# A hybrid decoder layer in fp32: the value half of the up weights is loaded into the other ring of weight buffers

## The chip, the core and the metric

The kernel runs on one core of one Trainium2 chip. The metric is device time in microseconds (us) of one execution; lower is better. All times below come from the timed runs or from one profiled execution. In the rows PE is TensorE, PEld its weight loads, DVE is VectorE, ACT is ScalarE, POOL is GpSimd, and SP is SyncE, which issues all DMAs here.

## What is computed

One decoder layer on 1024 tokens of width 1024: three token mixers (forgetting attention, a short gated convolution, a gated delta rule), merged into the residual, then a channel mixer, then a gated embedding per layer. The change touches the channel mixer alone:

```python
u = causal_dwconv(rmsnorm(x, g_ffn) @ w_up, ffn_conv_w)   # width 3, D_FF = 2816
u_gate, u_val = jnp.split(u, 2, axis=-1)
x = x + (jax.nn.silu(u_gate) * u_val) @ w_down
```

## The kernel before, in words

Activations lie transposed, 128 channels by 1024 tokens to a tile. Products run in two parts: each fp32 operand is split into a high part (a copy on ScalarE, L129) and a low part (a subtraction, L130, mostly on VectorE), and each product is three matmuls: high by high, high by low, low by high. A weight tile so split stands in the ring "wo" (5 buffers).

The up projection works through 22 pairs f of one gate tile and one value tile of 128 output channels each. The weights of a tile are 128 x 1024 fp32, 512 KB. Pairs 0 and 1 use the plain product (`plain`). Pairs 2 to 21 use a product by seven (`seven`, Strassen-Winograd's): the gate tile holds the blocks a11 and a12, the value tile a21 and a22, and `stationary` forms four sums of them,

- s1 = a21 + a22 on GpSimd, s2 = s1 - a11 on VectorE, s3 = a11 - a21 on GpSimd, s4 = a12 - s2 on VectorE (all L199),

in a ring "ws" of 3 buffers of 512 columns. Seven weights go to TensorE: a11 (product 1), a12 (2), s4 (3), a22 (4), s2 (6), s3 (7), s1 (5). A block of the loop takes seven products of 12 matmuls: in program order product 1 of the new pair, 3 of the old pair, 2 new, 4 old, then 6, 7, 5 new. So a22 and s4 of a pair are used a block later than its other weights. Results are evacuated on ScalarE (L213, L217, L227, L230) and VectorE (L220, L223, L231). When a pair is complete, `gated` runs the convolution's taps (L1092 on ScalarE, L1094 on VectorE), the sigmoid (L1125), the gate's product (GpSimd, L1126) and the value's (VectorE, L1128), and stores the activation tile to DRAM (L1133). Pairs 2 and 3 stay in SBUF.

Two rings of weight buffers of 128 x 1024 fp32 matter here:

- "wq", 3 buffers, filled by `wpair` (L192): in the up projection gate and value tile of each pair in turn, so a tile takes the buffer of the third tile before it. After the up projection `wpair` reads activations back (`fetch`).
- "wr", 2 buffers, filled by `wraw` (L136): the weights of all other products, the embedding's (wple) before the up projection and the down projection's (wdn) after it. In the up projection nothing uses it.

A buffer can be filled again when the last reader of its tile is done. For the value tile that is the split of a22; for the gate tile it is s4, which reads a12.

The order of instructions on each engine's queue isn't written by hand: a planner lays it out when the kernel is built, from modelled times of all instructions, in program order where two are ready. Each engine, SyncE's DMA queue too, then runs its own queue in that order and waits where an operand or a buffer isn't ready.

Of the kernel before, what the change touches and what calls it, by code (L numbers as in the profile page):

```python
# [17 lines left out]
NF = 22  # L18
# [30 lines left out]
def hybrid_block(ctx: ExitStack, tc: tile.TileContext, I, out, dbg=None):  # L49
    nc = tc.nc  # L50
    dbg = dbg or {}
    V, S, G, Q = nc.vector, nc.scalar, nc.gpsimd, nc.sync
    uid = [0]

    def nm(s):
        uid[0] += 1
        return f"{s}_{uid[0]}"
# [8 lines left out]
    @contextmanager  # L66
    def phase(name, psum=None, **roles):

        with ExitStack() as es:
            def pool(n, **k):  # L70
                return es.enter_context(tc.tile_pool(name=n, bufs=1, reuse_waits="tile", **k))
            sb = pool(name)
            ps = pool(name + "p", space=bass.MemoryType.PSUM) if psum else None
            old = dict(homes)
            homes.update({r: (sb, n) for r, n in roles.items()})
            homes.update({r: (ps, n) for r, n in (psum or {}).items()})
            scopes.append(sb)
            yield
            scopes.pop()
            homes.clear()  # L80
            homes.update(old)

    def pt(tag, bufs, w=512, dt=F32):
        pool, n = homes.setdefault(tag, (scopes[-1], bufs))
        return pool.tile([P, w], dt, tag=tag, name=nm(tag), bufs=n)
# [33 lines left out]
    def col(i):  # L119
        return cols[:, i : i + 1]  # L120
# [7 lines left out]
    def split(h, l, x, eng=None):  # L128
        S.activation(h, x, AF.Copy)  # L129
        (eng or V).tensor_tensor(out=l, in0=x, in1=h.bitcast(F32), op=ALU.subtract)  # L130
# [3 lines left out]
    def wraw(src, n=1024):  # L134
        wr = wp.tile([P, 1024], F32, tag="wr", name=nm("wr"), bufs=WR)
        Q.dma_start(wr[:, :n], src)  # L136
        return wr

    def wsplit(x, eng):

        m = x.shape[-1]
        w = wp.tile([P, 1024], F32R, tag="wo", name=nm("wo"), bufs=WO)
        h, l = w[:, 0:m], w[:, 512 : 512 + m]
        split(h, l, x, eng)
        return h, l

    def wload(src, n=1024, eng=None):
        wr = wraw(src, n)
        return [wsplit(wr[:, c : min(c + 512, n)], eng or weng[0]) for c in range(0, n, 512)]
# [26 lines left out]
    def operand(x, new):  # L176

        o = new()
        split(o[:, 0:512], o[:, 512:1024], x)
        return o  # L180

    def moving_sums(b1, b2, new, eng):

        x11, x12, x21, x22 = b1[:, NB[0]], b1[:, NB[1]], b2[:, NB[0]], b2[:, NB[1]]
        t3, t2, t4 = (pt("u", 4) for _ in range(3))
        for e, o, x, y in zip(eng, (t3, x12, t2, t4), (x22, x12, x22, x21), (x12, x11, x12, t2)):
            (G if e == "g" else V).tensor_tensor(out=o, in0=x, in1=y, op=ALU.subtract)
        return {6: operand(t2, new), 5: operand(x12, new), 7: operand(t3, new), 4: operand(t4, new)}

    def wpair(src, n=1024):  # L190
        w = pt("wq", 3, 1024)
        return w, Q.dma_start(w[:, :n], src).ins  # L192

    def stationary(a, b, m):

        a11, a12, a21, a22 = a[:, 0:m], a[:, m : 2 * m], b[:, 0:m], b[:, m : 2 * m]
        s1, s2, s3, s4 = (pt("ws", 3)[:, 0:m] for _ in range(4))
        for e, o, x, y, op in zip(SUMS, (s1, s2, s3, s4), (a21, s1, a11, a12), (a22, a11, a21, s2), (ALU.add,) + (ALU.subtract,) * 3):
            (G if e == "g" else V).tensor_tensor(out=o, in0=x, in1=y, op=op)  # L199
        return {k: lambda x=x, e=e: wsplit(x, G if e == "g" else V)  # L200
                for k, x, e in zip((1, 4, 2, 6, 3, 7, 5), (a11, a22, a12, s2, s4, s3, s1), SUBS)}
# [32 lines left out]
    def plain(ws, xs, outs):  # L234

        ps = [mmb() for _ in range(4)]
        for k in range(8):
            kt, half = k // 2, k % 2
            for m in range(2):
                wh, wl = ws[2 * m + half]  # L240
                sl = slice(kt * P, kt * P + P)
                for nb in range(2):
                    x = xs[half, nb][kt]
                    h, l, o = x[:, 0:512], x[:, 512:1024], ps[2 * m + nb]
                    mm(o, wh[:, sl], h, k == 0, False)
                    mm(o, wh[:, sl], l, False, False)
                    mm(o, wl[:, sl], h, False, k == 7)
        for o, p in zip(outs, ps):
            S.activation(o, p, AF.Copy)
# [698 lines left out]
    def xgt():  # L948
        return xp.tile([P, T], F32R, tag="xg", name=nm("xg"))

    def big(dt=F32):
        return pt("a", 16, T, dt)

    with phase("la", psum=dict(mm=6, sm=2), a=16, wq=3):
        with phase("me", tmp=9, sg=4, yr=4):
# [50 lines left out]
            for b in range(3):  # L1006
# [5 lines left out]
                for d2 in range(4):  # L1012
# [8 lines left out]
                    w = wload(I["wbr"][4 * b + d2])  # L1021
# [67 lines left out]
        with phase("up"):  # L1089
            def taps(cv, c0):  # L1090
                o = pt("o", 3, T)
                S.activation(o, cv[:, 0:T], AF.Copy, scale=col(c0))  # L1092
                for i in (1, 2):
                    V.scalar_tensor_tensor(out=o, in0=cv[:, i : i + T], scalar=col(c0 + i), in1=o,  # L1094
                                           op0=ALU.mult, op1=ALU.add)
                return o

            stored = []

            def padded():  # L1100
                cs = pt("cg", 2, T + 4), pt("cw", 2, T + 4)
                for c in cs:
                    G.memset(c[:, 0:2], 0.0)
                return cs

            def spans(*cs):
                return [c[:, 2 + 512 * nb : 514 + 512 * nb] for c in cs for nb in range(2)]

            acts, ahead = {}, {}

            def fetch(f):
                acts[f], ins = wpair(adr[f])
                return ins

            def gated(f, cg, cv):
                if f == NF - 1:
                    with tc.issue_after(stored[-1]):
                        for g in GROUPS[1][:3]:
                            fetch(g)
                        for dt in range(8):  # L1120
                            ahead[dt] = big()
                            Q.dma_start(ahead[dt], x2dr[dt])
                o = taps(cg, C_FF + 3 * f)
                sg = cg[:, 2 : T + 2]
                S.activation(sg, o, AF.Sigmoid)  # L1125
                G.tensor_tensor(out=sg, in0=o, in1=sg, op=ALU.mult)  # L1126
                o = taps(cv, C_FF + 3 * (NF + f))
                V.tensor_tensor(out=o, in0=o, in1=sg, op=ALU.mult)  # L1128
                if f in KEPT:
                    acts[f] = xgt(), xgt()  # L1130
                    split(*acts[f], o)
                else:
                    stored.append(Q.dma_start(adr[f], o).ins)  # L1133

            def up(f):
                w = stationary(wpair(I["wup"][f])[0], wpair(I["wup"][NF + f])[0], 512)
                cg, cv = padded()
                return w, spans(cg, cv), lambda: gated(f, cg, cv)

            halves = {(h, nb): [] for h in range(2) for nb in range(2)}  # L1140
            for k in range(4):
                for h in range(2):
                    x = x2s[k + 4 * h]
                    V.scalar_tensor_tensor(out=x, in0=x, scalar=col(C_G2 + k + 4 * h), in1=rs2, op0=ALU.mult, op1=ALU.mult)
                    for nb in range(2):
                        halves[h, nb].append(operand(x[:, NB[nb]], xgt))
            xs = {1: halves[0, 0], 2: halves[1, 0], 3: halves[1, 1], 4: [], 5: [], 6: [], 7: []}
            for f in range(PLAIN):
                cg, cv = padded()
                if f:  # L1150
                    wa, wb = wpair(I["wup"][f])[0], wpair(I["wup"][NF + f])[0]
                    first = [wsplit(x, V) for x in (wa[:, 0:512], wa[:, 512:1024], wb[:, 0:512], wb[:, 512:1024])]
                plain(first, halves, spans(cg, cv))
                gated(f, cg, cv)
                for k in (2 * f, 2 * f + 1):
                    for i, t in moving_sums(x2s[k], x2s[k + 4], lambda: big(F32R), "vvvv").items():
                        xs[i].append(t)
            seven([lambda f=f: up(f) for f in range(PLAIN, NF)], xs)

        with phase("do", tmp=8, sg=4):  # L1160
# [11 lines left out]
            for g in GROUPS:  # L1172
                for f in g:
                    act(f)
                n = len(g)
                for d2 in range(4):
                    w = wload(I["wdn"][:, c0 : c0 + 256 * n], 256 * n)
# [101 lines left out]
```

## Time and profile before

| | us |
|---|---|
| median of 3 runs | 1984.83 (1982.81 to 1985.93) |
| profiled execution | 1983.83 |
| its span, first to last instruction | 1981.7 |
| TensorE busy in it | 1938.0 |
| VectorE busy in it | 1337.2 |

The span lies inside the profiled execution's time. The seven-product loop stands from about 1251 to 1652 us. The granted clock of TensorE is 0.997 of full speed over the span.

### The profile page before, as it was taken

To read this page: it belongs to the slowest core of one execution; us is meant where nothing else is said; L and a number is where in the kernel's file an instruction comes from. 1 tells how busy PE (TensorE), PEld (TensorE's weight loads), DVE (VectorE), ACT (ScalarE), POOL (GpSimd) and SP (SyncE) were. 2 spreads that over 40 slices of the span, in tenths; PEclk is the share of its full clock that TensorE was granted. 3 is DMA by queue.
4 is the path that set the end of the run, shared out by engine and by line. 5 is a ranking of instruction groups with operands and counts; after the bars stand their busy time and mean duration, and the time that the engine had idled before them with its cause. 6 is when DMAs were issued, how large, how long until landed. Compare 5 with 4: busy or idle time off the path is not lost. (4 is left out here: it accounts for less than half of the span.)

```text
span 1981.7 us, 25403 instructions
## 1 busy us (share of the span) xinstructions
PE 1938.0 (98%) x9281; PEld 1608.2 (81%) x9281; DVE 1337.2 (67%) x2161; ACT 907.7 (46%) x1651; POOL 526.8 (27%) x431
## 2 busy tenths in 40 slices
PE   8999999999999999999999999999999999999998
PEld 6888888888888888888788787777777778888887
DVE  6878788878487123348757439888788888444564
ACT  6576777677422233333424336444444444111351
POOL 1445334434322222100044011334343430000200
PEclk9999999999999999999999999999999999999999
DMA  4221112221432144357853432121212127322132
GB/s 178 70 90 67 59 59 71 68 74 65 151 111 91 62 136 138 98 209 252 300 182 128 181 109 94 58 70 64 96 64 97 64 75 274 105 88 86 43 117 85
DMA packets 102636, 219.40 MB, mean 111 GB/s; under 512 B 9360, under 2 KB 40432, under 8 KB 102512
## 3 DMA queue, kind: packets, MB, share of 16 engines
q1 hardware_dynamic: 102512, 217.79, 32.4%
q8 instruction: 73, 1.20, 0.3%
q14 instruction: 51, 0.42, 0.1%
HBM read 158.98 MB, written 58.77 MB: 110 GB/s over the span
## 5 line engine op out<-in xcount | busy, mean ns | idle before, releaser
L126 PE MATMUL mm<-xg,wo 128*128 128x512 f32 x6128 | 1486.3, 393 | 18.4 <-DVE wo L130 12.3
L126 PEld LDWEIGHTS mm<-xg,wo 128*128 128x128 f32 x6128 | 1140.8, 188 | 262.1 <-DVE wo L130 19.5
L126 PE MATMUL mm<-a,wo 128*128 128x512 f32 x1216 | 303.6, 389 | 1.4 <-DVE sg L1029 1.4
L126 PEld LDWEIGHTS mm<-a,wo 128*128 128x128 f32 x1216 | 228.4, 188 | 49.7 <-DVE sg L1029 1.8
L129 ACT ACTIVATE wo<-wr 128x512 fp32r<-128x512 f32 x232 | 144.6, 626 | 267.3 <-PE mm L126 257.7
L130 POOL TENSOR_TENSOR wo<-wr,wo 128x512 fp32r<-128x512 f32 x108 | 149.8, 1390 | 312.8 <-ACT wo L129 301.8
L1181 DVE TENSOR_TENSOR a<-mm,a 128x512 f32<-128x512 f32 x96 | 65.2, 687 | 91.6 <-PE mm L126 91.4
L130 DVE TENSOR_TENSOR wo<-wr,wo 128x512 fp32r<-128x512 f32 x124 | 89.4, 723 | 28.0 <-ACT wo L129 27.4
L280 POOL TENSOR_TENSOR tmp<-tmp,tmp 128x512 f32<-128x512 f32 x21 | 28.1, 1339 | 293.4 <-ACT tmp L278 281.8
L1030 POOL TENSOR_TENSOR a<-a,sg 128x512 f32<-128x512 f32 x28 | 42.4, 1520 | 191.9 <-DVE sg L1029 191.9
L130 DVE TENSOR_TENSOR wo<-wq,wo 128x512 fp32r<-128x512 f32 x68 | 79.2, 1166 | 3.2 <-ACT wo L129 3.2
L1094 DVE SCALAR_TENSOR_TENSOR o<-cw,cols,o 128x1024 f32<-128x1024 f32 x44 | 77.8, 1768 | 0.0
L491 DVE SCALAR_TENSOR_TENSOR o<-cv,cols,o 128x512 f32<-128x512 f32 x72 | 69.9, 970 | 10.1 <-ACT o L489 9.1
L503 ACT ACTIVATE o<-mm 128x512 f32<-128x512 f32 x60 | 35.7, 595 | 89.4 <-PE mm L126 53.3
L129 ACT ACTIVATE wo<-ws 128x512 fp32r<-128x512 f32 x80 | 50.2, 631 | 56.8 <-PE mm L126 56.7
L600 ACT ACTIVATE pp<-pp,small 128x512 f32<-128x512 f32 (+2 forms) x96 | 58.4, 610 | 28.0 <-DVE small L594 27.6
L1126 POOL TENSOR_TENSOR cg<-o,cg 128x1024 f32<-128x1024 f32 x22 | 55.6, 2525 | 39.4 <-ACT cg L1125 39.4
L199 POOL TENSOR_TENSOR ws<-wq 128x512 f32<-128x512 f32 x20 | 29.9, 1494 | 122.6 <-DMA wq<-wup 121.4
L1092 ACT ACTIVATE o<-cw,cols 128x1024 f32<-128x1024 f32 x22 | 25.4, 1156 | 74.8 <-DVE cw L223 74.8
L130 DVE TENSOR_TENSOR pl<-pq,ph 128x512 fp32r<-128x512 f32 (+1 forms) x80 | 49.9, 628 | 13.9 <-ACT ph L129 13.5
L199 POOL TENSOR_TENSOR ws<-wq,wq 128x512 f32<-128x512 f32 x20 | 43.7, 2186 | 56.3 <-DVE wo L130 52.3
L199 DVE TENSOR_TENSOR ws<-ws,wq 128x512 f32<-128x512 f32 x20 | 14.9, 745 | 64.3 <-POOL ws L199 64.3
(291 smaller groups left out, 2453.4 us busy)
## 6 DMA issues: line engine op xcount, KB each, us to landing
wr<-win SPq DMA_DIRECT2D x64, 512.0 KB, 3.6
wq<-wup SPq DMA_DIRECT2D x44, 512.0 KB, 3.5
r<-o SPq DMA_DIRECT2D x64, 256.0 KB, 2.6
ad<-o SPq DMA_DIRECT2D x20, 512.0 KB, 3.9
wq<-ad SPq DMA_DIRECT2D x20, 512.0 KB, 4.4
wr<-wdn SPq DMA_DIRECT2D x20, 512.0 KB, 3.7
yr<-r SPq DMA_DIRECT2D x16, 512.0 KB, 5.1
sg<-r SPq DMA_DIRECT2D x32, 256.0 KB, 3.4
```

The costliest lines, as they stand in the source:

```text
L126: pe[0] = nc.tensor.matmul(o, lhsT=l, rhs=r, start=start, stop=stop, skip_group_check=more)
L129: S.activation(h, x, AF.Copy)
L130: (eng or V).tensor_tensor(out=l, in0=x, in1=h.bitcast(F32), op=ALU.subtract)
L199: (G if e == "g" else V).tensor_tensor(out=o, in0=x, in1=y, op=op)
L280: eng[nb].tensor_tensor(out=acc[nb], in0=acc[nb], in1=sq, op=ALU.add)
L491: V.scalar_tensor_tensor(out=o, in0=cv[:, i : i + 512], scalar=col(c0 + i), in1=o, op0=ALU.mult, op1=ALU.add)
L503: S.activation(o, ps, AF.Copy)
L600: S.activation(t[:, :w], t[:, :w], AF.Exp, bias=mn[:, k - 1 : k], scale=-1.0, accum_out=sm[:, i : i + 1])
L1030: (V if b == 2 and dt > 5 else G).tensor_tensor(out=m, in0=m, in1=t, op=ALU.add)
L1094: V.scalar_tensor_tensor(out=o, in0=cv[:, i : i + T], scalar=col(c0 + i), in1=o, op0=ALU.mult, op1=ALU.add)
L1126: G.tensor_tensor(out=sg, in0=o, in1=sg, op=ALU.mult)
L1181: V.tensor_tensor(out=x2[dt][:, NB[nb]], in0=ps, in1=x2[dt][:, NB[nb]], op=ALU.add)
```

## The change

The value tile of each pair from 2 to 21 is loaded by `wraw` into the ring "wr" instead of by `wpair` into the ring "wq"; the gate tile stays in "wq". Pairs 0 and 1 are loaded as before. `wpair` loses a parameter that no caller used. No buffer is added to either ring, and the sums, splits and products are the same.

```diff
-    def wpair(src, n=1024):
+    def wpair(src):
         w = pt("wq", 3, 1024)
-        return w, Q.dma_start(w[:, :n], src).ins
+        return w, Q.dma_start(w, src).ins
@@
             def up(f):
-                w = stationary(wpair(I["wup"][f])[0], wpair(I["wup"][NF + f])[0], 512)
+                w = stationary(wpair(I["wup"][f])[0], wraw(I["wup"][NF + f]), 512)
                 cg, cv = padded()
                 return w, spans(cg, cv), lambda: gated(f, cg, cv)
```

## Rows read from the trace of the kernel before

**Rows 1.** Page, busy time by engine: us, share of the span, instructions.

```profile
PE 1938.0 (98%) x9281; PEld 1608.2 (81%) x9281; DVE 1337.2 (67%) x2161; ACT 907.7 (46%) x1651; POOL 526.8 (27%) x431
```

**Rows 2.** Windows: stretch, length, busy us (instructions), granted clock, DMA share, GB/s.

```profile
1251.60:1273.33 21.73, 18.49 (x74) 14.49 (x72) 15.77 (x15) 7.34 (x13) 9.01 (x7) 0.92 0.18 66
1273.33:1292.37 19.04, 19.04 (x86) 15.77 (x84) 16.80 (x17) 10.13 (x15) 7.13 (x7) 1.00 0.20 60
...
1312.42:1631.26 318.84, 309.54 (x1345) 251.01 (x1344) 258.01 (x256) 146.85 (x224) 123.44 (x97) 1.00 0.22 78
```

**Rows 3.** Timeline of PE, one block: start, length, form, [idle before <-releaser].

```profile
1411.70 8.32 PE L126 MATMUL mm<-a,wo 128*128 128x512 f32 x36
...
1425.30 0.61 PE L126 MATMUL mm<-xg,wo 128*128 128x512 f32 x2
...
1426.42 5.28 PE L126 MATMUL mm<-xg,wo 128*128 128x512 f32 x22 [0.51 <-DVE wo L130]
```

**Rows 4.** Timeline of the same block: DVE, POOL and SP's queue.

```profile
1411.79 0.69 DVE L199 TENSOR_TENSOR ws<-wq,ws 128x512 f32<-128x512 f32 x1
...
1412.55 15.98 SPq L192 DMA_DIRECT2D wq<-wup  x2
...
1416.12 1.28 POOL L199 TENSOR_TENSOR ws<-wq 128x512 f32<-128x512 f32 x1 [4.91 <-DMA wq<-wup]
1417.44 0.69 DVE L199 TENSOR_TENSOR ws<-ws,wq 128x512 f32<-128x512 f32 x1 [3.70 <-POOL ws L199]
...
1423.89 2.48 DVE L130 TENSOR_TENSOR wo<-wq,wo 128x512 fp32r<-128x512 f32 x1
...
1427.49 0.68 DVE L130 TENSOR_TENSOR wo<-wq,wo 128x512 fp32r<-128x512 f32 x1
...
1429.33 0.33 SPq L1133 DMA_DIRECT2D ad<-o  x1
...
1431.65 0.69 DVE L199 TENSOR_TENSOR ws<-wq,ws 128x512 f32<-128x512 f32 x1
```

**Rows 5.** Waits, 1240 to 1680 us: waiter <- releaser: us, times, longest.

```profile
PE mm L126 <- DVE wo L130: 12.3, 17, 3.0
```

**Rows 6.** Groups by form, 1312 to 1632 us: busy us, mean ns | idle before.

```profile
L130 DVE TENSOR_TENSOR wo<-wq,wo 128x512 fp32r<-128x512 f32 x48 | 61.7, 1285 | 0.0
L1094 DVE SCALAR_TENSOR_TENSOR o<-cw,cols,o 128x1024 f32<-128x1024 f32 x32 | 57.5, 1798 | 0.0
L1126 POOL TENSOR_TENSOR cg<-o,cg 128x1024 f32<-128x1024 f32 x16 | 41.9, 2616 | 5.2 <-ACT cg L1125 5.2
L1094 DVE SCALAR_TENSOR_TENSOR o<-cg,cols,o 128x1024 f32<-128x1024 f32 x32 | 40.9, 1279 | 0.0
L130 DVE TENSOR_TENSOR wo<-ws,wo 128x512 fp32r<-128x512 f32 x48 | 40.7, 848 | 0.0
...
L199 POOL TENSOR_TENSOR ws<-wq,wq 128x512 f32<-128x512 f32 x16 | 36.4, 2276 | 51.2 <-DVE wo L130 51.2
...
L130 POOL TENSOR_TENSOR wo<-ws,wo 128x512 fp32r<-128x512 f32 x17 | 22.6, 1331 | 7.6 <-ACT wo L129 7.6
...
L199 POOL TENSOR_TENSOR ws<-wq 128x512 f32<-128x512 f32 x16 | 20.6, 1288 | 78.9 <-DMA wq<-wup 78.9
```

**Rows 7.** The up loads of line 192, 1312 to 1632 us: issue to landing.

```profile
DMA to landing us min/median/max: 3.3/3.6/4.1
```

**Rows 8.** Timeline at the start of the loop.

```profile
1233.29 1.76 DVE L199 TENSOR_TENSOR ws<-ws,wq 128x512 f32<-128x512 f32 x1 [1.18 <-POOL ws L199]
...
1263.38 3.68 PE L126 MATMUL mm<-xg,wo 128*128 128x512 f32 x8 [3.01 <-DVE wo L130]
```

**Rows 9.** Timeline around the end of the loop.

```profile
1176.84 0.33 SPq L136 DMA_DIRECT2D wr<-wdn  x1
...
1636.79 0.69 DVE L130 TENSOR_TENSOR wo<-wq,wo 128x512 fp32r<-128x512 f32 x1
...
1649.85 2.88 PE L126 MATMUL mm<-a,wo 128*128 128x512 f32 x12
```

## Prediction

> **What bounds the kernel now.** I read the busy table first: TensorE is busy 98% of the span [rows 1], so the whole kernel has 44 us of TensorE idleness to give back, and only what lies in the stage that the diff touches counts. Next I cut that stage, the seven-product loop of the up projection, into stretches [rows 2]. A product is 12 matmuls; five of them, without a hole, fill the 13.60 us from 1411.70 to 1425.30 [rows 3], so one product is 2.72 us and one block of seven is 19.04 us. The stretch of one block from 1273.33 lasts exactly that: a block without loss. The 16 blocks from 1312.42 to 1631.26 last 318.84 us, 19.93 each, so each loses 0.89 us, 14.2 us in all.
>
> Where a block loses it stands in the timeline of TensorE [rows 3]: two matmuls at 1425.30, which end their turn at 1425.75, then a hole of 0.7 us until VectorE has made the low half of a weight (1426.42, released by DVE wo L130). The list of waits names the same releaser, 17 times [rows 5]. So I asked why VectorE is late, and read its own timeline with those of GpSimd and SyncE [rows 4]. Call the block whose sums are made there f. VectorE makes s4 of block f-1 at 1411.79; this is the last read of the gate tile of f-1, and only now (1412.55) SyncE can issue the value load of f into its buffer. GpSimd stands idle 4.91 us for that load, makes s1 at 1416.12, and VectorE, which runs its queue in order, stands idle 3.70 us at s2 (1417.44) with three taps, an evacuation and two weight splits queued behind it, the last of them the one that TensorE needs. That split is the one at 1423.89.
>
> This is a loop: s4 on VectorE, load, s1 on GpSimd, s2 on VectorE, all other work of VectorE, the next s4. Its length is VectorE's work plus the idle time: 258.01 us over 16 blocks [rows 2] is 16.13 of work, and 19.93 less that leaves 3.8, which is the idle time at s2. TensorE needs 19.04 and gets 19.93: VectorE's loop, not TensorE, sets the pace.
>
> **The change part by part.** *Value loads in the other ring.* Removed: the value half's place in the three-buffer ring wq. Added: a place in the two-buffer ring wr. No instruction is added, none grows; the 44 up loads stay 512 KB each on SyncE's queue. What moves is the event that frees the buffer. Today the value tile of f+1 takes the buffer of the gate tile of f, freed by s4 of f (1431.65 to 1432.34). Changed, it takes the value buffer of f-1, last read by the split of its second half on VectorE, at 1427.49 [rows 4], which ends at 1428.17. That is 4.2 us earlier. A load of this stage lands in 3.3 to 4.1 us [rows 7], so it is there by 1432.3. The sum s1 of f+1 also needs a buffer of the three-deep ring ws, freed by the same s4, at 1432.34. The load is thus hidden behind a wait that exists anyway, and what is late next is s4 itself.
>
> From there GpSimd needs 1.29 us [rows 6], so s1 ends at about 1433.7. VectorE meanwhile has two pieces of about 0.6 us after s4 (an evacuation, a split of the next gate tile) and is free at about 1433.6. Its idle time falls from 3.8 us to some 0.2; its loop would be 16.13 + 0.2 = 16.3 us, under TensorE's 19.04, and the 0.89 us vanishes. With VectorE ahead by up to 3.6 us, the hole of 0.7 us at 1425.75 closes with 2.9 us to spare.
>
> What can eat that margin, bounded by rows: s1 no longer runs while VectorE is idle. At best it costs nothing; at worst VectorE is held for the whole 1.29 us and s1 itself grows to the 2.28 us of the equal sum s3 that runs beside VectorE [rows 6], 1.0 more. The loop is then 16.13 + 1.29 + 0.2 + 1.0 = 18.6, still under 19.04. I take 14.2 us of gain, and 0 for the worst, since no end crosses 19.04 by itself. If besides the planner puts the value load behind the activation store (issued at 1429.33 [rows 4], 1.1 us after the buffer is free, landing by about 1433.4), 0.9 us more would give 19.5, and only 0.43 of the 0.89 us would be won: a gain of 6.9. This is the low end.
>
> *Gate loads.* With the ring wq to themselves the gate tiles run three blocks deep: the load of f+2 is free to go at s4 of f-1, a whole block before use. Cost nothing, covered by some 19 us of lead. The two loads in a block simply swap places on SyncE's queue: the slot just ahead of the store is today a gate load's, and it still lands within 4.1 us [rows 7], so the store that follows it does not hold it up much.
>
> *Start of the loop.* From 1251.60 to 1273.33, six products (16.32 us) take 21.73: 5.4 us lost, 3.01 of them in one hole [rows 2, 8]. Here VectorE is full with the two plain blocks' taps and moving sums and waits for GpSimd's first sum only 1.18 us [rows 8], so an early value load can give at least 0, at most 5.4; nearest is the 1.18, and I take 1.2. The block between 1292.37 and 1312.42, the ends of its neighbours, lasts 20.05, 1.0 over [rows 2]; it waits in the same loop, I take 1.0 (0 to 1.0).
>
> *End of the loop and the down projection.* Today two down-projection weights sit in wr some 460 us ahead of use, the later one issued at 1176.84 [rows 9]. In the changed kernel the value tiles hold wr until the end, so the second of these loads waits for the split of the last value tile, today at 1636.79 [rows 9]. Issued at 1637.5 it lands by 1641.6, is split 1.3 us later, and its matmuls come after those at 1649.85: nothing lost. If the planner leaves that split until TensorE needs it, at 1649.85, the weight is ready at 1649.85 + 3.6 + 1.3 = 1654.8, and TensorE, done at 1652.57, waits 2.2 us. I take 0; bounds 0 and 2.2, no gain.
>
> **Sum.** 14.2 + 1.0 + 1.2 = 16.4 us. The profiled execution took 1983.83 us (span 1981.7, 2.1 around it): 1967.4. The median of the runs is 1.0 above it, so 1968.4.
>
> **The rivals.** *Part of it comes back* (chance 0.13): the load queued behind the store, or a planner's order in which VectorE still waits a microsecond or two. The time by the low end above: 14.2 shrinks to 6.9, the start gives 0, the end costs 0 to 2.2: 1984.8 - 6.9 + 2.2 = 1980 down to 1974. For it: the order is made by a planner from modelled times that I do not see. Against: the slot in which the load would stand is used today without delay.
>
> *Nothing changes* (0.09): the planner, knowing the load early, puts s1 or s2 elsewhere and VectorE waits as long for something else, for instance s3, for which GpSimd already idles 51.2 us over 16 blocks, 3.2 each, behind VectorE [rows 6]. VectorE's loop stays near 19.9 and the time near 1984.8. Against: no other row makes VectorE wait in a steady block; it idles once.
>
> *Slower, by VectorE and GpSimd holding each other up* (0.07). VectorE's work of 16.13 us already holds some of this: splits from wq average 1285 ns where an undisturbed one is 0.68, taps of cw 1798 where those of cg take 1279, splits from ws 848 [rows 6]. Over a block that is 3 x 0.60 + 2 x 0.52 + 3 x 0.17 = 3.35 us, beside 6.22 us of GpSimd (2.28 + 2.62 + 1.33): about half. Undisturbed, VectorE would need 12.8. With s1 all four GpSimd pieces, 7.5 us, would lie beside VectorE. Were it held for all of them, the loop would be 20.3, 0.37 over today, 16 times: +5.9, so 1990.7. It decides from the point where VectorE is held for more than 19.93 - 12.8 = 7.1 of those 7.5 us. Against: half, not all, is what the rows show.
> The Trainium skill's "SBUF — State Buffer" (section "SBUF: two separate sides") says that these two engines share one pair of ports under an exclusive lock, and that the one that comes second blocks for the whole instruction. By that rule alone this rival would be the forecast; the half that the trace shows goes against reading it so strictly.
>
> **How the numbers follow.** Forecast 0.71, 1964 to 1974: its best end takes all of the start, 14.2 + 1.0 + 5.4 = 20.6 off 1984.8, so 1964.2. The range reaches down to 1963 and up over the partial case to 1979; outside stay the unchanged and the slower case and a little below, under 2 in 10. A measurement of this kernel can tell about 0.2%, 4 us, from no change. Faster by more: 0.71 and 0.13, 0.84; same 0.09; slower 0.07.
>
> **What the changed profile would show.** Right: the idle time of GpSimd before ws<-wr L199 released by a load gone, or released by VectorE; VectorE's idle time before s2 under 1 us; blocks of 19.04 in TensorE's timeline and no hole after two matmuls; value loads issued right behind the split of the second half. Wrong: blocks still near 19.9 with VectorE busy for more than 18 us of each (held by GpSimd), or idle elsewhere (a new wait), or a hole of several us at the first down-projection weights. The whole fails if the hole after two matmuls stays though VectorE no longer waits at s2.

## The result and the profile after

| | before | after |
|---|---|---|
| median, us | 1982.81 (run beside it) | 1967.19 |
| ratio after to before, 95% interval | | 0.9913 (0.9900 to 0.9927) |
| profiled execution, us | 1983.83 | 1967.07 |
| its span, us | 1981.7 | 1965.1 |

The medians differ by 15.6 us, which is 0.79%; the ratio, with its interval, says 0.87%. Four of the five runs of the changed kernel lie between 1966.51 and 1967.22; a fifth, of 3942.92, is left out of the ratio. The spans differ by 16.6 us. The page's busy table after:

```profile
PE 1930.3 (98%) x9281; PEld 1605.9 (82%) x9281; DVE 1331.0 (68%) x2161; ACT 910.8 (46%) x1651; POOL 531.9 (27%) x431
```

Windows of the stretches that answer to those of before [rows 2]: start to the first three products of the second pair, the block that lost 1.0, and the 16 steady blocks (stretch, length, busy of PE, PEld, DVE, ACT, POOL with instructions, granted clock, DMA share, GB/s).

```profile
1250.68:1270.41 19.73, 17.27 (x74) 13.28 (x72) 15.33 (x15) 6.23 (x11) 6.89 (x6) 1.00 0.15 54
1289.45:1308.49 19.04, 19.04 (x86) 15.77 (x84) 16.04 (x17) 10.12 (x15) 7.79 (x6) 1.00 0.14 51
1308.49:1613.13 304.64, 304.64 (x1346) 252.25 (x1344) 254.63 (x258) 150.10 (x224) 120.21 (x97) 1.00 0.23 79
```

The 16 steady blocks last 304.64 us, 19.04 each, and TensorE is busy in all of it: 14.20 us less than before. The start, from the loop's first product to these blocks, shrank from 60.82 to 57.81 (3.01 less). The loop begins 0.92 earlier, and the stretch behind the 16 blocks is 1.53 longer (351.97 against 350.44). Together: 14.20 + 3.01 + 0.92 - 1.53 = 16.6. No run says where the 0.92 ahead of the loop comes from.

One steady block in the timeline of TensorE, which answers to [rows 3] (start, length, form, count):

```profile
1403.69 8.32 PE L126 MATMUL mm<-a,wo 128*128 128x512 f32 x36
1411.85 2.43 PE L126 MATMUL mm<-xg,wo 128*128 128x512 f32 x10
1414.11 2.88 PE L126 MATMUL mm<-a,wo 128*128 128x512 f32 x12
1416.83 6.06 PE L126 MATMUL mm<-xg,wo 128*128 128x512 f32 x26
```

The group that was cut after two matmuls is whole: 26 matmuls without a hole. The same stretch on VectorE, GpSimd and SyncE's queue, which answers to [rows 4]:

```profile
1396.48 0.68 DVE L130 TENSOR_TENSOR wo<-wr,wo 128x512 fp32r<-128x512 f32 x1
1397.19 0.33 SPq L136 DMA_DIRECT2D wr<-wup  x1
1398.32 0.33 SPq L1133 DMA_DIRECT2D ad<-o  x1
1400.87 0.69 DVE L199 TENSOR_TENSOR ws<-wq,ws 128x512 f32<-128x512 f32 x1
1401.64 0.33 SPq L192 DMA_DIRECT2D wq<-wup  x1
1401.70 1.29 POOL L199 TENSOR_TENSOR ws<-wr 128x512 f32<-128x512 f32 x1 [3.25 <-DVE ws L199]
1402.95 1.29 POOL L130 TENSOR_TENSOR wo<-ws,wo 128x512 fp32r<-128x512 f32 x1
1404.28 0.69 DVE L199 TENSOR_TENSOR ws<-ws,wq 128x512 f32<-128x512 f32 x1 [2.11 <-POOL wo L130]
1405.04 0.69 DVE L130 TENSOR_TENSOR wo<-wq,wo 128x512 fp32r<-128x512 f32 x1
```

The value load goes out at 1397.19, right behind the split of the old pair's a22 (1396.48). GpSimd no longer waits for it here: s1 at 1401.70 is released by VectorE's s4. But VectorE still stands idle 2.11 us at s2 (1404.28), now for a split on GpSimd. That split takes the old pair's s1; the planner has put it behind the new pair's s1, where before it stood ahead of it. (s2 needs one of the three buffers of "ws"; by its releaser it gets the one that this split reads.) VectorE's own order has changed in a block too: the split of the next gate tile (1405.04) now stands behind s2, where before it stood ahead of it, and the evacuation of L231 has moved ahead of a split. The waits from 1240 to 1680 us, which answer to [rows 5] (waiter, releaser: us, times, longest):

```profile
POOL ws L199 <- DVE ws L199: 46.3, 15, 4.9
...
DVE ws L199 <- POOL wo L130: 36.6, 17, 2.8
...
POOL ws L199 <- DMA wr<-wup: 6.5, 2, 3.9
...
PE mm L126 <- DVE wo L130: 2.1, 1, 2.1
```

TensorE's 12.3 us of waiting for VectorE's splits have become 2.1, in the single hole at the start. VectorE's loop, work plus wait at s2, is 254.63 / 16 = 15.91, plus 2.11: 18.0 us, under TensorE's 19.04.

### The profile page after: what moved, and what is told of

It is laid out like the page before. It is cut to its first block, busy times and chain, and to the rows that moved or that the text cites. A ratio compares the mean times of both kernels' runs of the same rounds, so it can differ in the third digit from the quotient of the medians.

```text
span 1965.1 us, 25454 instructions
## 1 busy us (share of the span) xinstructions
PE 1930.3 (98%) x9281; PEld 1605.9 (82%) x9281; DVE 1331.0 (68%) x2161; ACT 910.8 (46%) x1651; POOL 531.9 (27%) x431
## 4 chain that ended last, share of the span: by engine, by line
PE 75%; DVE 11%; DMA 5%; ACT 4%; issue 3%; POOL 1%; SPq 0%; DVEq 0%; ACTq 0%; POOLq 0%
PE mm L126 65%; PE sm L126 5%; DVE o L491 1%; DMA sg<-r 1%; PE py L126 1%; PE ev L126 1%; PE pq L637 1%; DVE wo L130 1%; DMA kc<-kdr 1%; DMA y<-yr 1%; DVE o L1094 1%; PE po L126 1%; DMA yr<-r 1%; DVE pl L130 1%; ACT pp L600 1%
## 5 line engine op out<-in xcount | busy, mean ns | idle before, releaser
L129 ACT ACTIVATE wo<-wr 128x512 fp32r<-128x512 f32 x252 | 157.2, 626 | 278.0 <-PE mm L126 269.9
L130 DVE TENSOR_TENSOR wo<-wr,wo 128x512 fp32r<-128x512 f32 x144 | 106.6, 742 | 27.9 <-ACT wo L129 27.4
L130 DVE TENSOR_TENSOR wo<-wq,wo 128x512 fp32r<-128x512 f32 x48 | 65.4, 1365 | 5.0 <-ACT wo L129 4.2
L199 POOL TENSOR_TENSOR ws<-wq,wr 128x512 f32<-128x512 f32 x20 | 44.0, 2199 | 78.9 <-DVE wo L130 73.9
L1094 DVE SCALAR_TENSOR_TENSOR o<-cg,cols,o 128x1024 f32<-128x1024 f32 x44 | 58.4, 1327 | 5.0 <-ACT o L1092 4.9
L199 POOL TENSOR_TENSOR ws<-wr 128x512 f32<-128x512 f32 x20 | 35.9, 1797 | 72.3 <-DVE ws L199 46.3
L637 PE MATMUL pq<-cst,pp 128*128 128x128 f32 x288 | 47.0, 273 | 2.0 <-DVE pl L130 1.1
```

Of the source, the lines that this page charges most:

```text
L637: nc.tensor.transpose(pq[:, c : c + P], pr[s][kt // 4][:, kt % 4 * P : kt % 4 * P + P], ident)
```

## The experiments

All run beside the kernel before, and each ratio is to that. Times are medians. Three questions: is it VectorE's wait that cost, is it the load's lateness that made the wait, and how much room does the changed kernel have?

### Is the loss VectorE's wait at s2?

The rings stay as before; s2 moves from VectorE to GpSimd, so that GpSimd waits for the load and VectorE's queue runs on.

```diff
-WR, WO, SUMS, SUBS = 2, 5, "gvgv", "vvvvvvg"
+WR, WO, SUMS, SUBS = 2, 5, "gggv", "vvvvvvg"
```

> The kernel before, its loads and rings untouched, with s2 = s1 - a11 made on GpSimd instead of VectorE. The rest of VectorE's queue keeps its order. Theory (the loss is VectorE standing in its queue at s2, waiting for a load; not the load's lateness in itself): GpSimd waits now, VectorE does not, blocks of 19.04 us, 14 to 16 us faster than before: 1966 to 1969. Rival (the value load must come earlier): GpSimd still starts s1 when the load lands, the block stays near 19.9, 1983, or worse by GpSimd's slower subtraction (1.3 us against 0.7).

Measured 1966.51, ratio 0.9907 (0.9893 to 0.9922); blocks of 19.04 (1309.49 to 1328.53 and on). GpSimd's timeline in a steady block:

```profile
1407.07 1.28 POOL L199 TENSOR_TENSOR ws<-wq 128x512 f32<-128x512 f32 x1 [2.62 <-DMA wq<-wup]
1408.44 2.17 POOL L199 TENSOR_TENSOR ws<-ws,wq 128x512 f32<-128x512 f32 x1
```

GpSimd still waits 2.62 us for a value load as late as ever, and the whole gain is there. The rest of VectorE's order in a steady block is that of the kernel before but for one exchange: the evacuation of L231 and a split have swapped places. A late load costs nothing by itself here; what stood in VectorE's queue behind s2 paid for it.

Next, VectorE's loop made longer: in the kernel before s2 is made four times.

```diff
-            (G if e == "g" else V).tensor_tensor(out=o, in0=x, in1=y, op=op)
+            [(G if e == "g" else V).tensor_tensor(out=o, in0=x, in1=y, op=op) for _ in range(4 if o is s2 else 1)]
```

> The kernel before, with s2 made four times instead of once in each block (the same values into the same buffer), three more subtractions of 0.6 us on VectorE. Theory: VectorE's loop sets the block, so 1.8 us a block, 19.93 to 21.7, 29 to 31 us over 16 to 17 blocks: about 2013 us. Rival (TensorE's waits come from the order, VectorE has 3.7 us idle in a block and can take them): within 5 us of 1983.

Measured 2018.01, ratio 1.0166 (1.0148 to 1.0185). VectorE's wait at the first s2 of a pair is unchanged, so the added work is paid in full and a little more:

```profile
1428.47 0.69 DVE L199 TENSOR_TENSOR ws<-ws,wq 128x512 f32<-128x512 f32 x1 [3.84 <-POOL ws L199]
...
1438.67 5.30 PE L126 MATMUL mm<-xg,wo 128*128 128x512 f32 x22 [1.84 <-DVE wo L130]
...
1460.55 6.90 PE L126 MATMUL mm<-xg,wo 128*128 128x512 f32 x22 [1.84 <-DVE wo L130]
```

The little more is in the last two rows: behind some of TensorE's holes the same 22 matmuls take 6.90 us in place of 5.30 (last section). Between 1340 and 1600 us that happens five times, some 8 us of the 34.

The third run fell outside both ranges. In the kernel before the value tile is loaded twice, one load behind the other.

```diff
-                w = stationary(wpair(I["wup"][f])[0], wpair(I["wup"][NF + f])[0], 512)
+                g, v = wpair(I["wup"][f])[0], wpair(I["wup"][NF + f])[0]; Q.dma_start(v, I["wup"][NF + f]); w = stationary(g, v, 512)
```

> The kernel before, with the value tile of each pair from 2 to 21 loaded twice into the same buffer, the second load behind the first. Theory (the value load is a link of VectorE's loop): a second load of 3.6 us is added to a block of 19.93, so 23.5 us a block, 57 to 62 us over the 16 to 17 steady blocks, about 2043 us. Rival (the planner's order of the instructions made the gain, the load's time is hidden): within 5 us of the kernel before, 1983.

Measured 1989.16, ratio 1.0034 (1.0022 to 1.0047): 6.7 us over the kernel before, where the theory had some 60 and the rival at most 5. GpSimd waits 7.67 us for the load where it waited 4.91 [rows 4], VectorE at s2 no longer than before:

```profile
1421.52 1.29 POOL L199 TENSOR_TENSOR ws<-wq 128x512 f32<-128x512 f32 x1 [7.67 <-DMA wq<-wup]
1422.85 1.76 DVE L199 TENSOR_TENSOR ws<-ws,wq 128x512 f32<-128x512 f32 x1 [3.59 <-POOL ws L199]
```

The planner lays out the second load too. It has put two taps, an evacuation and a split more ahead of s2 in VectorE's queue, and they fill the longer wait. VectorE's wait is thus not the load's length alone, but what is left of it behind the work that the planner put there. The run doesn't part the theory from its rival, since it changes the order too.

### Is it the load's lateness that makes the wait?

The same second load in the changed kernel. Here the order on PE, VectorE, ScalarE and GpSimd stays as in the changed kernel; SyncE's queue alone differs.

```diff
-                w = stationary(wpair(I["wup"][f])[0], wraw(I["wup"][NF + f]), 512)
+                g, v = wpair(I["wup"][f])[0], wraw(I["wup"][NF + f]); Q.dma_start(v, I["wup"][NF + f]); w = stationary(g, v, 512)
```

> The changed kernel, value tiles loaded twice; the queues of the four compute engines hold the same instructions in the same order as in the changed kernel. Theory: the change shortened the loop rather than cut it. It now runs from the split of the second value half over the load (3.9), s1 and VectorE's work to the next such split, 14.2 to 14.5 us without the load; with the load 18.4, some 0.6 under TensorE's 19.04. Twice the load gives 22.0 to 22.3 us a block, 48 to 60 us more than the changed kernel: 2015 to 2027 us. My prediction's own picture, in which s4 is what is late and the load has only a microsecond to spare but VectorE 2.9, would give less, up to 1990. Rival (planner's order): 1967, since the order is the same.

Measured 2008.24, ratio 1.0129 (1.0115 to 1.0143), 41 us over the changed kernel and 7 under the range of the theory. A block lasts 21.6 us (43.18 for two). GpSimd waits for the load again, VectorE for GpSimd:

```profile
1422.30 1.29 POOL L199 TENSOR_TENSOR ws<-wr 128x512 f32<-128x512 f32 x1 [6.32 <-DMA wr<-wup]
...
1424.88 0.69 DVE L199 TENSOR_TENSOR ws<-ws,wq 128x512 f32<-128x512 f32 x1 [5.92 <-POOL wo L130]
```

With the order fixed, only the load's lateness has changed, so it is what makes the wait. The second load goes out 3.83 us behind the first (1418.55 after 1414.72); 21.6 less 3.83 is 17.8, what the way over the load would take in the changed kernel if TensorE did not hold it up.

The same with s2 on GpSimd as well (the two edits above together):

> The changed kernel with the value tiles loaded twice (2008 us as it stood) and s2 on GpSimd. Theory: the load lands 7.6 us after its issue as there, but nobody whom TensorE needs soon waits for it: s1 and s2 end about 9 us ahead of the split of s2 that product 6 needs. Near the changed kernel, 1967 to 1971. Rival (the load's lateness costs by itself): near 2008.

Measured 1971.85, ratio 0.9941 (0.9924 to 0.9958). GpSimd waits up to 7.3 us for the load, and the blocks are 19.04 again; of the 4.7 us over the changed kernel 3.4 lie ahead of the steady blocks, which begin that much later. So 36 of the 41 us were VectorE's wait.

Then the rings the other way round: gate in "wr", value in "wq", where it has three buffers to itself.

```diff
-                w = stationary(wpair(I["wup"][f])[0], wraw(I["wup"][NF + f]), 512)
+                w = stationary(wraw(I["wup"][f]), wpair(I["wup"][NF + f])[0], 512)
```

> The two halves exchanged: the gate tile in the ring of two, the value tile in the ring of three. Theory: the value tile now takes the buffer of the pair three before it, free a whole block earlier, and the gate tile that of the pair two before it, freed by s4 a block before its use; both loads are out of the loop, blocks of 19.04 us, and the time that of the changed kernel, 1965 to 1969 us. Rival (planner's order): anything between 1967 and 1983.

Measured 1967.17, ratio 0.9926 (0.9912 to 0.9939): the same as the changed kernel, since both run at TensorE's 19.04. And with the value tile loaded twice on top:

> As the exchanged kernel, with the value tiles loaded twice. Theory: the load has some 19 us to spare there, so a second one of about 4 us costs nothing: within 3 us of the exchanged kernel, some 1967 us. If a load costs time by itself (traffic, SyncE's queue, the store that waits behind it), it shows here: up to 16 x 3.6, 2025 us.

Measured 1970.25, ratio 0.9937 (0.9924 to 0.9951): blocks of 19.04, 3.1 us over the kernel without the second load, where the same load cost the changed kernel 41. What helps is that the value's buffer comes free early, and the earlier the more lateness it bears; the ring's name doesn't matter. A fourth buffer in "wq" was not tried.

### How much room does the changed kernel have?

By VectorE's busy time of 15.9 in a block of 19.04 there seemed to be some 3 us. First s2 made nine times in the changed kernel (the edit of above with 9):

> The changed kernel with s2 made nine times, eight more subtractions, 4.8 us of VectorE a block. Theory: VectorE has some 2.9 us to spare there, so 1.9 us a block show, blocks of about 20.9, 30 to 36 us more than the changed kernel: 1997 to 2003 us. If VectorE's loop were as tight as before the change, all 4.8 would show: 77 to 82 us, 2045.

Measured 2027.52, ratio 1.0219 (1.0204 to 1.0235): 24 us over the theory's range and 18 under the 2045 of a loop as tight as before. Blocks of 21.89, and VectorE has no idle time left in them (21.75 busy). The counterpart to the kernel before with three more sums, at 4:

> The changed kernel with s2 made four times in each pair (three sums more on VectorE, 0.55 to 0.6 us each by the same edit to the kernel before, which cost that kernel 34 us). Theory: in the changed kernel TensorE sets the pace and VectorE has room, 15.9 us of work in a block of 19.04, so 1.7 us more are hidden: 1967 to 1971. Rival: the loop over the buffer (split of a22, load, s1, s2, 11.9 us of other work of VectorE, next split), about 18.4 us, has 0.6 us of room alone; then blocks of 20.1 and 1983 to 1987.

Measured 1979.95, ratio 0.9977 (0.9966 to 0.9987): near the rival. Blocks of 19.66. The load, s1, and s2 behind GpSimd's split:

```profile
1427.54 0.33 SPq L136 DMA_DIRECT2D wr<-wup  x1
...
1431.54 1.30 POOL L199 TENSOR_TENSOR ws<-wr 128x512 f32<-128x512 f32 x1 [2.74 <-DMA wr<-wup]
...
1434.12 0.69 DVE L199 TENSOR_TENSOR ws<-ws,wq 128x512 f32<-128x512 f32 x1 [2.35 <-POOL wo L130]
```

GpSimd waits for the load again, and VectorE, 17.37 us busy, waits 2.35 at s2: 19.7. So the loop is there as before, only shorter; 19.66 less the added 1.8 is 17.9, in line with the 17.8 above and with 18.0 from the rows of after. So the room is about 1.0 to 1.2 us, not 3.

Three more of s4 in place of s2 (`4 if o is s4`) put the same work beside the load:

> The changed kernel with s4 made four times in each pair: three sums more on VectorE (1.8 us), at another place than three more s2. Theory: VectorE's own queue is still a loop in the changed kernel, its work plus the 2.1 us that it waits at s2 for two pieces of GpSimd (the new pair's s1 and the split of the old pair's s1); 15.9 + 2.1 leaves 1.0 us of room, so 1.8 more make blocks of 19.7 to 19.9 and 1977 to 1982. Rival: only the way over the load of the value tile binds; s4 lies beside that load, so blocks of 19.04 to 19.3 and 1967 to 1972.

Measured 1976.19, ratio 0.9961 (0.9948 to 0.9975), just under the theory's range. But its reason was wrong. A window over 14 blocks:

```profile
1328.16:1600.59 272.43, 270.87 (x1177) 219.65 (x1176) 269.73 (x268) 128.44 (x196) 108.47 (x84) 1.00 0.23 79
```

VectorE doesn't wait at s2; it is busy 19.27 us of a block of 19.46, 3.4 more than in the changed kernel, for 1.8 us of work. Four rows show where the rest came from:

```profile
1423.32 1.30 POOL L130 TENSOR_TENSOR wo<-ws,wo 128x512 fp32r<-128x512 f32 x1 [0.28 <-ACT wo L129]
1423.41 2.36 DVE L130 TENSOR_TENSOR wo<-ws,wo 128x512 fp32r<-128x512 f32 x2
...
1425.89 1.30 POOL L199 TENSOR_TENSOR ws<-wr 128x512 f32<-128x512 f32 x1 [1.27 <-DMA wr<-wup]
...
1426.29 3.63 DVE L199 TENSOR_TENSOR ws<-wq,ws 128x512 f32<-128x512 f32 x4
```

Two splits of 0.68 us each take 2.36 under GpSimd's split. Of the four sums, 3.63 us, the last three take 0.7 each and the first 1.45, where one alone takes 0.69: it was held until GpSimd's s1 was done. Whether VectorE waits for GpSimd's two pieces or is held under them comes to much the same. By that reading the time should not fall without the wait at s2 (s2 on GpSimd, s4 five times). The theory put there, written before the result above, says that it does:

> The changed kernel with s2 on GpSimd and s4 made five times: VectorE has as much work as with three more s4 (one sum off, four on), but no instruction of it waits for GpSimd at s2. Theory: without that wait its 17.7 us fit into 19.04: 1966 to 1971. Rival: VectorE's work, stretched by GpSimd, is what costs: 1977 to 1985, as with s2 on VectorE.

Measured 1995.38, ratio 1.0057 (1.0041 to 1.0073): the theory failed, and the rival fell short by 10 us. VectorE waits for nothing and is busy 40.50 of 40.77 us in two blocks. GpSimd's s2 is a fifth piece of work that holds it: a tap of cg that began under it took 2.32 us, with s2 on VectorE 1.28. The cure would be less work on GpSimd, even at the price of more on VectorE: s3 and the split of s1 moved to VectorE, with s4 made four times.

```diff
-WR, WO, SUMS, SUBS = 2, 5, "gvgv", "vvvvvvg"
+WR, WO, SUMS, SUBS = 2, 5, "gvvv", "vvvvvvv"
```

> The changed kernel with s4 made four times, and s3 and the split of s1 moved from GpSimd to VectorE: VectorE gets five instructions more than in the changed kernel and two more than with three more s4 alone, GpSimd keeps s1 and the gate's product. Theory: what VectorE lacks is held by GpSimd's two-input instructions, each of which makes an instruction of VectorE that starts under it wait for its end; the two taken off GpSimd save VectorE 1.05 and 1.1 us and cost it 0.6 each, so its time in a block falls from about 19.5 to 18.6, under TensorE's 19.04: 1966 to 1971. Rival: VectorE's number of instructions is what counts; 1.2 us more than 19.5 makes blocks of 20.7 and 1993 to 1999.

Measured 1966.33, ratio 0.9917 (0.9892 to 0.9941). A window over 14 blocks:

```profile
1324.27:1590.83 266.56, 266.56 (x1178) 220.72 (x1177) 262.38 (x298) 129.67 (x196) 65.07 (x57) 1.00 0.23 82
```

Blocks of 19.04; VectorE does two instructions more per block than in the window above and is busy 18.74 us, 0.5 less (expected: 18.6). So it is the time for which GpSimd holds VectorE, and not the number of VectorE's instructions, that decided here.

## Why the prediction was right, and where its steps were not

*The loss and its place.* Right: 14.2 us for 16 blocks was forecast and 14.20 measured. The block ahead of them gave the 1.0 that was taken (20.05 to 19.04). That the whole sum came so near, 16.4 forecast and 16.6 between the spans, is in part luck: 0.8 more at the start and 0.92 ahead of the loop were not forecast, and the 1.53 lost behind the blocks, not forecast either, offsets them.

*The cause.* Right, and shown: with the late load left in place and s2 off VectorE's queue the whole gain appears; with the early load made late again in an unchanged order the loss returns, more than twice over (41 us against 15.6).

*The load.* Right: it goes out right behind the split of the old a22 and is hidden behind s4. It is ahead of the store, not behind it (1397.19 and 1398.32), so the low end of the range did not come into play. Its landing from 1290 to 1632 us, with the first loads of wdn among them, answers to [rows 7]:

```profile
DMA to landing us min/median/max: 2.6/3.7/5.0
```

*VectorE's idle time at s2.* Wrong. The forecast was 0.2 us, and a loop of 16.3; the rows show 2.11 and 18.0. The step that failed is "GpSimd needs 1.29 us, so s1 ends at about 1433.7": it counted s1 alone between s4 and s2, and two pieces of VectorE to cover it. The planner put GpSimd's split of the old s1 there too, 1.29 us more, and s2 waits for that; and of VectorE's two pieces it left only the evacuation there, with the split of the next gate tile, 0.6, behind s2 (1405.04). The 0.2 forecast and these two make the 2.1 measured. It cost nothing because 18.0 is still under 19.04; the worst case of 18.6 that the prediction carried along was nearer than its best value, though by another way than it named: s1 itself takes 1.29 us, as before. "Under 1 us of idle time at s2", named as a sign of being right, was therefore the wrong sign. The right one was that the sum of work and idle time stays under 19.04.

*Gate loads.* Nothing was forecast and nothing shows: none of the waits over 0.2 us from 1240 to 1680 names a load of wq from wup.

*The start.* 1.2 us were taken for the first stretch, with bounds of 0 and 5.4; 2.0 measured (21.73 to 19.73). The hole of 3.01 us shrank to 2.14 [rows 8]. The rest is TensorE's clock, which the prediction had not looked at (a granted clock of 0.92 in this stretch [rows 2]; last section).

*The end.* The displaced loads of wdn cost nothing, as forecast. But a hole of 1.27 us stands there that wasn't in the sum. TensorE and ScalarE:

```profile
1636.32 1.65 PE L126 MATMUL mm<-xg,wo 128*128 128x512 f32 x6 [1.27 <-ACT cg L217]
...
1633.42 1.06 ACT L129 ACTIVATE xg<-wq 128x1024 fp32r<-128x1024 f32 x1 [8.10 <-DMA wq<-ad]
```

ScalarE ran late because it stood 8.10 us before the first activation read back into wq, and the evacuation that TensorE waited for was queued behind that. The fetches went out from 1626.14 on, 7.3 us ahead of the use. With the gate tiles in "wr", which displaces the same loads of wdn, the hole is absent and the fetch lands in 5.4 us. That the change causes it is not shown; it looks like a spread of the landing.

*The rivals.* That part comes back or nothing changes: did not happen; both hung on VectorE waiting elsewhere, and it does, but 1 us too little to matter. The slower rival, by VectorE and GpSimd holding each other up, priced all of GpSimd's 7.5 us against VectorE. In the changed kernel VectorE isn't held more than before (15.91 busy against 16.13), since s1 and the split of the old s1, 2.58 of the 7.5, lie in its idle time at s2. The mechanism itself is real, and takes over as soon as the idle time is filled: VectorE with three more s4 needs 12.8 (the prediction's undisturbed figure) + 1.8 = 14.6 and is busy 19.27, so it is held for some 4.7 of GpSimd's 7.75 us (108.47 / 14). The prediction said that the half in the rows goes against reading the exclusive lock strictly. That conclusion was wrong. Five rows of the changed kernel, GpSimd's first:

```profile
1408.64 2.27 POOL L199 TENSOR_TENSOR ws<-wq,wr 128x512 f32<-128x512 f32 x1 [4.39 <-DVE wo L130]
1411.47 2.38 POOL L1126 TENSOR_TENSOR cg<-o,cg 128x1024 f32<-128x1024 f32 x1 [0.56 <-ACT cg L1125]
```

```profile
1408.48 1.28 DVE L1094 SCALAR_TENSOR_TENSOR o<-cg,cols,o 128x1024 f32<-128x1024 f32 x1
1409.67 2.32 DVE L1094 SCALAR_TENSOR_TENSOR o<-cw,cols,o 128x1024 f32<-128x1024 f32 x1
1411.91 2.48 DVE L130 TENSOR_TENSOR wo<-wq,wo 128x512 fp32r<-128x512 f32 x1
```

s3 ends at 1410.91; the tap that began under it ends at 1411.99, about its own 1.2 us later. The gate's product ends at 1413.85; the split that began under it ends at 1414.39, about its own 0.6 later. Both run as if they began when GpSimd's was over, and so they do in each of the 16 blocks (1.08 and 0.55 us after GpSimd's end). This is what the Trainium skill's "SBUF — State Buffer" (section "SBUF: two separate sides") says of VectorE's instructions with two inputs in SBUF, that of the two engines the one that starts first has the ports for its whole instruction, and the trace agrees. A VectorE instruction with one input in PSUM isn't held. In the kernel before, under GpSimd's split, the evacuation of L231, which reads a product from PSUM, takes its bare 0.68 us, and the split behind it, both inputs in SBUF, 1.18:

```profile
1409.89 1.32 POOL L130 TENSOR_TENSOR wo<-ws,wo 128x512 fp32r<-128x512 f32 x1 [0.28 <-ACT wo L129]
```

```profile
1409.97 0.68 DVE L231 TENSOR_TENSOR cw<-mm,u 128x512 f32<-128x512 f32 x1
1410.58 1.18 DVE L130 TENSOR_TENSOR wo<-ws,wo 128x512 fp32r<-128x512 f32 x1
```

The half comes from elsewhere: where GpSimd begins under VectorE, GpSimd waits (s3 began under the tap of 1408.48 and takes 2.27 us, s1 of the same size 1.29), and where VectorE has idle time, nobody does.

## What to carry to other kernels

Where an in-order engine waits for something that its own earlier instruction set going, add up its work and the wait, and compare the sum with what the next engine needs: that, not the wait, says what an earlier load is worth. An equal time afterwards doesn't show how near the next loop is; a little work added on purpose does (here 1 us of room, where the busy time promised 3). And when pieces are moved to GpSimd to relieve VectorE, count their time against VectorE's instructions with two inputs in SBUF, wherever VectorE has no idle time to cover them.

## What the hardware showed beside

The hole at the start of the loop is followed in the kernel before by a slower TensorE, in the changed one not. Windows of before, during and after its hole of 3.01 us:

```profile
1261.40:1263.40 2.00, 0.02 (x1) 0.02 (x1) 2.00 (x3) 0.00 (x0) 1.42 (x2) 1.00 0.45 186
1263.40:1265.00 1.60, 1.60 (x4) 1.31 (x5) 1.13 (x2) 0.00 (x0) 0.00 (x0) 0.53 0.35 110
1265.00:1267.00 2.00, 2.00 (x6) 1.52 (x6) 0.00 (x0) 0.00 (x0) 0.00 (x0) 0.52 0.69 250
1267.00:1269.00 2.00, 2.00 (x11) 1.64 (x10) 0.00 (x0) 0.00 (x0) 0.00 (x0) 1.00 0.00 0
```

and of after, behind its hole of 2.14 us:

```profile
1262.00:1264.00 2.00, 1.98 (x9) 1.63 (x10) 1.17 (x2) 0.00 (x0) 0.00 (x0) 1.00 0.40 127
```

Before, the granted clock is 0.53 and 0.52, its level of 1.2 GHz, for some 3.6 us, and eight matmuls take 3.68 us [rows 8]; after, it stays at 1.00, and eight take 2.12. So a hole shortened by 0.87 us gave 0.87 + 1.56 = 2.4, of which 0.4 were lost again elsewhere in the stretch. The hole's length alone doesn't say which level follows: in the kernel before with three more sums, the two holes of 1.84 us shown there, in the same place of a block, are followed by different levels: a granted clock of 1.00 from 1438.67 to 1440.30, and of 0.58 from 1460.55 to 1462.20. So the 1.56 us can't be counted on from a shorter hole.

GpSimd is held by VectorE as well. With eight more sums VectorE's queue runs without a gap, and GpSimd's s3, 2.27 us in the rows above, took 5.76:

```profile
1420.44 5.76 POOL L199 TENSOR_TENSOR ws<-wq,wr 128x512 f32<-128x512 f32 x1 [3.08 <-issue]
...
1424.97 0.68 DVE L231 TENSOR_TENSOR cw<-mm,u 128x512 f32<-128x512 f32 x1
```

It ended at 1426.20, 1.23 us after VectorE began the evacuation that reads from PSUM; a sum of this size takes GpSimd 1.29 alone. All that VectorE ran from 1420.44 to 1424.97 has two inputs in SBUF.
